# A two-layer hybrid decoder trunk: another start, 32 modulation tiles in another stage, and other buffers around the FFN

## The chip, the cores and the metric

The kernel runs on one core of a Trainium2 chip. A core has five engines with a queue each: TensorE (PE, matrix products), VectorE (DVE), ScalarE (ACT), GpSimd (POOL) and SyncE (SP, which here issues every DMA). Each engine takes its instructions strictly in the order in which they stand in its queue, and a wait stops all that stands behind it. PE writes to PSUM (eight banks of 128 x 512 fp32), the other data lies in SBUF. The metric is the device time of one execution in microseconds (us).

## The reference

All of it is fp32: 1024 tokens of width 1024, two layers, then a last RMSNorm.

```python
for l in range(DEPTH):
    mod = c_act @ ada_w[l] + ada_b[l]              # c_act = silu(c), one row
    shift1, scale1, gate1, shift2, scale2, gate2 = split(mod, 6)
    h = rms_norm(x, norm1_g[l]) * (1.0 + scale1) + shift1
    z = h @ w_in[l]                                # q | k | v | GLU input | two gates
    o = subln(diff_attention(rope(q), rope(k), v)) # 4 heads, two softmaxes each, causal
    y_attn = o @ w_attn_o[l]
    u = silu(layer_norm(conv31(ga * sigmoid(gb))))
    y_conv = u @ w_conv_o[l]
    x = x + (1 + gate1) * ((sig(g_attn)*y_attn + sig(g_conv)*y_conv) @ w_out[l])
    h2 = rms_norm(x, norm2_g[l]) * (1.0 + scale2) + shift2
    f_gate, f_up = split(h2 @ w_ffn_in[l], 2)      # 2 x 2816 columns
    x = x + (1 + gate2) * ((silu(f_gate) * f_up) @ w_ffn_out[l])
return rms_norm(x, final_g)
```

## The kernel before

Activations are kept transposed: eight feature tiles (128 features x 1024 tokens), each worked in two halves of 512 tokens (`hf`). Every fp32 operand of a product is split into a rounded high part and the rest (ACT makes the high part, DVE or POOL subtracts it), and three products are summed in one PSUM bank: high x high, high x low of the activation, low of the weight x high. A weight slab is 128 x 1024 (512 KB): `wslab` loads it into one of two `wraw` buffers, ACT casts `wh`, POOL subtracts `wl` (L139 to L142). A 128 x 512 output of 1024 inputs is thus 24 matmuls of 512 columns.

**Order of the work.** The program is written stage by stage, and a scheduler with a timing model of its own fixes the order in each engine's queue before the launch. It may pull an instruction ahead where its model finds the engine free, and tile pools set which buffer must be free first.

**Start (L503 to L538), layer 0.** x is loaded; ACT squares each tile by halves; DVE (half 0) and POOL (half 1) add the eight squares (L515); PE sums over partitions with a column of ones (`rstd_diag`, L307, 8 matmuls of one column); POOL raises to the power -0.5 (L310); DVE makes four diagonal tiles per half and PE spreads the factor over partitions (L317). Then, feature tile by feature tile: two modulation tiles (`ada_col`: a 512 KB load, and on DVE a 128 x 1024 multiply with accumulation by `cs` = silu(c), L193, a bias add L194, and for scales and gates one more column instruction), x times the factor (L532, DVE or POOL), ACT scales and shifts (L534) and casts `hh` (L535), DVE subtracts `hl` (L536). After it the rope tables: range reduction of angles on POOL in 76 small instructions (`rope_tables`, L210), two Sin on ACT, three small stores.

**GLU (L567 to L579).** Four slabs, kept at once, are multiplied by half (`linear_half`: the 16 products with `wh`, then the 8 with `wl`), then four more. In layer 0 the remaining 32 modulation tiles (16 to 47: gate1, shift2, scale2, gate2) stand behind it (L577). Convolution on DVE (31 taps, L614, with its sum in PSUM), attention and gate projections follow as one plan.

**Mix (L706 to L764).** `branch` multiplies attention and convolution outputs by their slabs (48 matmuls per slab); DVE multiplies each bank by a sigmoid gate (L749), POOL adds the two branches (L759), ACT and DVE split the sum (L762, L763). `w_out` follows (L806), DVE adds to x and squares are summed (L810, L302).

**FFN (L776 to L951).** One Strassen-like step: `b1`..`b7` are seven 512-feature operands; DVE and POOL form differences of the quarter tiles (L826 to L828, L834) and split them (L784), half of the tiles on each. 22 groups f each load two rows of slabs (`wraw`, `fraw`, two buffers each), form weight sums on DVE (L866 to L869) and make seven products of 12 matmuls (L880, L881, L883). Each group writes two 256 KB pieces to DRAM (`gf`).

**Output product (L954 to L1041).** `gblock` reads `gf` back in pieces (`gs`, 256 KB, five buffers) and splits them; all six blocks of half 0 are asked for ahead of the loop (L994), then eight x tiles (L996). 48 steps follow (two halves, two groups of four outputs, six blocks, two slabs), each up to 24 matmuls. Behind each of the first 16 steps of layer 0 stand three of layer 1's 48 modulation tiles (`ada_next`, L1022). The pools for `gs` and half of the blocks (`GP`) lie where the FFN's pools lay.

## Time and profile before

| | us |
|---|---|
| three timed runs | 2988.03, 2985.60, 2981.32; median 2985.60 |
| profiled execution, its own time | 2990.07 |
| its span, first to last instruction | 2988.2 |
| PE / DVE / ACT / POOL busy in the span | 2783.1 / 1836.9 / 1158.0 / 1719.9 |
| PE instructions | 12544 |
| granted TensorE clock, mean share | 0.965 |
| DMA, mean over the span | 118 GB/s |

Times in a trace count from the span's first instruction. Matmuls are pipelined and their ends are modelled, so PE's busy time also holds stretches in which it runs slowly. How well PE is used in a stretch is seen by its matmuls: their count against the length of the stretch.

### The profile page before, as it was taken

How to read it: one execution, taken by the hardware profiler on the slowest of the kernel's cores; microseconds unless marked ns; L12 is line 12 of the kernel's file. 1: busy time of each engine (PE TensorE's matmuls, PEld its weight loads, DVE VectorE, ACT ScalarE, POOL GpSimd, SP SyncE). 2: the span in 40 equal slices, each digit the busy share in tenths (PEclk: the TensorE clock that was granted, in tenths of full speed). 3: DMA queues.
4: the chain of work that ended last, by engine and by line, in shares of the span. 5: the costliest groups of instructions: out<-in, count | busy, mean ns of one | idle time of the engine just before them, and what ended most of it. 6: DMA issues, size and time to landing. Idle time of an engine off the chain costs nothing. (4 is left out here: it accounts for less than half of the span.)

```text
span 2988.2 us, 35455 instructions
## 1 busy us (share of the span) xinstructions
PE 2783.1 (93%) x12544; PEld 2284.7 (76%) x12544; DVE 1836.9 (61%) x2997; ACT 1158.0 (39%) x2059; POOL 1719.9 (58%) x1256
## 2 busy tenths in 40 slices
PE   3899999899979999889899999998997999998998
PEld 2688788777758888667788888886875788886886
DVE  8889976554574466589618989545446644443222
ACT  4246544343433333332322565435334233333321
POOL 6957745334686666554542776642457666666643
PEclk9999999989989999999999999998998999999999
DMA  7621222335232222388432122132451322225442
GB/s 272 229 83 65 71 78 85 113 102 194 100 110 88 78 85 85 112 277 287 158 121 89 64 75 78 56 107 85 141 201 68 119 85 85 85 78 180 136 121 93
DMA packets 151952, 353.92 MB, mean 118 GB/s; under 512 B 15328, under 2 KB 28000, under 8 KB 151776
## 3 DMA queue, kind: packets, MB, share of 16 engines
q1 hardware_dynamic: 151776, 351.67, 34.7%
q8 instruction: 99, 1.62, 0.2%
q14 instruction: 77, 0.63, 0.1%
HBM read 282.30 MB, written 69.30 MB: 118 GB/s over the span
## 5 line engine op out<-in xcount | busy, mean ns | idle before, releaser
L142 POOL TENSOR_TENSOR wl<-wraw,wh 128x1024 fp32r<-128x1024 f32 (+1 forms) x216 | 513.0, 2376 | 587.1 <-ACT wh L141 391.2
L141 ACT CAST wh<-wraw 128x1024 fp32r<-128x1024 f32 (+1 forms) x216 | 219.5, 1017 | 404.5 <-PE pfo L1018 186.7
L784 POOL TENSOR_TENSOR wt<-wraw,wt 128x512 fp32r<-128x512 f32 x172 | 247.7, 1441 | 169.6 <-ACT wt L783 169.5
L1017 PE MATMUL pfo<-gh,wh 128*128 128x512 f32 x640 | 256.1, 402 | 31.1 <-ACT gh L783 22.8
L151 PE MATMUL pg<-hl,wh 128*128 128x512 f32 x640 | 253.0, 397 | 16.9 <-DVE hl L536 16.8
L614 DVE SCALAR_TENSOR_TENSOR pc<-uc,vec,pc 128x512 f32<-128x512 f32 x348 | 261.1, 750 | 6.0
L150 PE MATMUL pg<-hh,wh 128*128 128x512 f32 x640 | 253.8, 401 | 9.1 <-ACT hh L535 8.9
L1018 PE MATMUL pfo<-gl,wh 128*128 128x512 f32 x640 | 254.3, 397 | 0.0
L1019 PE MATMUL pfo<-gh,wl 128*128 128x512 f32 x640 | 243.0, 399 | 8.7 <-POOL wl L142 8.6
L783 ACT CAST wt<-wraw 128x512 fp32r<-128x512 f32 x172 | 106.9, 622 | 310.2 <-PE pf L883 259.2
L609 POOL TENSOR_TENSOR uc<-uc,ct 128x512 f32<-128x512 f32 x120 | 139.0, 1158 | 57.5 <-ACT ct L608 56.8
L1017 PEld LDWEIGHTS pfo<-gh,wh 128*128 128x128 f32 x640 | 124.1, 194 | 60.9 <-ACT gh L783 23.7
L154 PE MATMUL pg<-hh,wl 128*128 128x512 f32 x640 | 168.7, 395 | 0.0
L443 ACT ACTIVATE e<-psc,nb 128x512 f32<-128x512 f32 (+2 forms) x192 | 110.5, 579 | 145.9 <-DVE nb L440 113.1
L1019 PEld LDWEIGHTS pfo<-gh,wl 128*128 128x128 f32 x640 | 123.3, 193 | 42.1 <-POOL wl L142 16.5
L151 PEld LDWEIGHTS pg<-hl,wh 128*128 128x128 f32 x640 | 121.0, 189 | 44.2 <-DVE hl L536 21.1
L150 PEld LDWEIGHTS pg<-hh,wh 128*128 128x128 f32 x640 | 121.8, 191 | 33.5 <-ACT hh L535 9.4
L1028 DVE SCALAR_TENSOR_TENSOR x<-pfo,gcol,x 128x512 f32<-128x512 f32 x32 | 23.7, 745 | 196.0 <-PE pfo L1019 195.5
L1018 PEld LDWEIGHTS pfo<-gl,wh 128*128 128x128 f32 x640 | 123.2, 192 | 25.9
L154 PEld LDWEIGHTS pg<-hh,wl 128*128 128x128 f32 x640 | 117.5, 188 | 23.3
L784 POOL TENSOR_TENSOR wt<-fraw,wt 128x512 fp32r<-128x512 f32 x88 | 118.7, 1349 | 26.9 <-ACT wt L783 26.9
L438 DVE TENSOR_REDUCE mx<-psc 128x1 f32<-128x512 f32 (+2 forms) x192 | 102.7, 549 | 23.8 <-PE psc L437 16.0
(324 smaller groups left out, 7652.3 us busy)
## 6 DMA issues: line engine op xcount, KB each, us to landing
wraw<-in_w_ffn_out_dram SPq DMA_DIRECT2D x80, 512.0 KB
wraw<-in_w_in_dram SPq DMA_DIRECT2D x72, 512.0 KB
adraw<-in_ada_w_dram SPq DMA_DIRECT2D x48, 512.0 KB
adraw<-in_ada_w_dram SPq DMA_DIRECT2D x96, 256.0 KB
fraw<-in_w_ffn_in_dram SPq DMA_DIRECT2D x44, 512.0 KB
wraw<-in_w_ffn_in_dram SPq DMA_DIRECT2D x44, 512.0 KB
gs<-gf SPq DMA_DIRECT2D x88, 256.0 KB
gd<-graw SPq DMA_DIRECT2D x64, 256.0 KB
```

The source lines that it names most:

```text
L141: S.copy(wh, raw)
L142: G.tensor_tensor(wl, raw, wh.bitcast(F32), op=ALU.subtract)
L150: PE.matmul(ps, wh[:, wc], rhs(0, k, hf), start=(k == 0), stop=False)
L151: PE.matmul(ps, wh[:, wc], rhs(1, k, hf), start=False, stop=False)
L154: PE.matmul(ps, wl[:, wc], rhs(0, k, hf), start=False, stop=(k == nk - 1))
L443: S.activation(e[:, n0:n1], pss[b][:, 0:n1 - n0], AF.Exp, bias=nb, scale=0.125, accum_out=sx[:, 2 * b + c:2 * b + c + 1])
L609: G.tensor_tensor(acc, acc, t, op=ALU.add)
L614: E.scalar_tensor_tensor(pc if k + 1 < CONV_K else acc, u[:, k:k + HF], w, pc, op0=ALU.mult, op1=ALU.add)
L784: E.tensor_tensor(lo, src, hi.bitcast(F32), op=ALU.subtract)
L1017: PE.matmul(ps, wh[:, wc], bh[:, k % 4, :], start=(not seen[q] and k == k0), stop=False)
L1018: PE.matmul(ps, wh[:, wc], bl[:, k % 4, :], start=False, stop=False)
L1019: PE.matmul(ps, wl[:, wc], bh[:, k % 4, :], start=False, stop=(seen[q] == NB - 1 and k == k1 - 1))
```

## The change

Seven edits, all in `trunk`:

1. The start takes all eight PSUM banks as one pool `ps0`, closed before the convolution; the four other PSUM pools open behind it. `pos` and `invf` are loaded first and the rope tables are written first.
2. ACT squares a whole tile and PE sums it at once: 8 one-column matmuls per tile, 64 in all, into one bank (`pst`). The adds of squares are gone. One power on POOL for both halves.
3. `cs` is a PSUM tile (two banks). Multiplication by factor and scale is one DVE instruction (L532's product is gone); half 0 takes `hl` on DVE, half 1 on POOL.
4. Behind each feature tile the first three GLU slabs take their 18 matmuls in six banks; the fourth slab and its product come later.
5. Modulation tiles 16 to 47 of layer 0 move into the mix, eight ahead of each of its first four rounds, with a second silu(c) in SBUF and three load buffers.
6. FFN opening: differences, and all splits of `b3`..`b7`, on DVE.
7. A pool on the right side (`ffnr`) stays open from the FFN to the layer's end: a third buffer for the second row of slabs, the five `gs` buffers, and two blocks; block 0 of half 0 is written in front of the last three FFN groups. x tiles are read during the first steps, and one `ada_next` stands behind each step in place of three.

```diff
+    pst0 = ExitStack()
+    ps0 = pst0.enter_context(tc.tile_pool(name="pstart", bufs=1, space=PSUM, reuse_waits="tile"))
...
-    cs0 = silu_c(ap0, 7)
-    Sqs = [nt("Sq") for hf in range(2)]
+    rope_tables(ap0)
+    pst = ps0.tile([P, KT], F32, name="pst", tag="s", bufs=6, padded_shape=[P, HF])
     for j in range(KT):
...
+        t = ap0.tile([P, T], F32, tag="sqt", name="sqt", bufs=2)
+        S.activation(t, xs[j], AF.Square)
+        for q in range(KT):
+            PE.matmul(pst[:, q:q + 1], t[:, q * P:(q + 1) * P], ones[:, 0:1], start=(j == 0 and q == 0), stop=(j == KT - 1 and q == KT - 1))
+    cs0 = silu_c(ap0, 7, ps0.tile([P, D], F32, name="cs", tag="cs", bufs=1))
...
     for j in range(KT):
+        if j < NS:
+            ws.append(glu_slab(0, j, up))
         for t in (KT + j, j):
             ada_col(0, t, cs0, ap0, 7)
...
-            (G if hf else V).tensor_tensor(xj, xj, pbs[hf], op=ALU.mult)
+            V.scalar_tensor_tensor(t, xs[j][:, hs], acol[0][0][:, j:j + 1], pbs[hf], op0=ALU.mult, op1=ALU.mult)
+            if hf:
+                S.activation(t, t, AF.Identity, bias=bc)
+                S.copy(hh.at(j), t)
+                G.tensor_tensor(hl.at(j), t, hh.at(j).bitcast(F32), op=ALU.subtract)
+            else:
+                S.activation(hh.at(j), t, AF.Identity, bias=bc)
+                V.scalar_tensor_tensor(hl.at(j), t, bc, hh.at(j).bitcast(F32), op0=ALU.add, op1=ALU.subtract)
+        for i in range(len(ws)):
...
+                for k in range(done[i], j + 1):
...
+                    PE.matmul(ps, wh[:, wc], hh, start=(k == 0), stop=False)
+                    PE.matmul(ps, wh[:, wc], hl, start=False, stop=False)
+                    PE.matmul(ps, wl[:, wc], hh, start=False, stop=(k == KT - 1))
...
-        if l == 0:
-            for t in range(16, 48):
-                ada_col(0, t, cs0, ap0, 7)
...
+        ada_t = iter(range(16, 48 if l == 0 else 16))
+        if l == 0:
+            csb = silu_c(B, 3)
         for j0 in range(0, KT + 2, 2):
+            for t in itertools.islice(ada_t, 8):
+                ada_col(0, t, csb, B, 3)
...
-                split_into(MV[p][0][:, j % 4, :], MV[p][1][:, j % 4, :], x, V if hf and j % 2 else G)
+                split_into(MV[p][0][:, j % 4, :], MV[p][1][:, j % 4, :], x, V if hf else G)
...
-            E = (V, G)[jj % 2]
+            E = V
...
-                split_into(MV[p][0][:, jj, :], MV[p][1][:, jj, :], x, V if jj % 2 else G)
+                split_into(MV[p][0][:, jj, :], MV[p][1][:, jj, :], x, V)
         xpool.close()
+        rst = ExitStack()
+        R = rst.enter_context(pool("ffnr", side="right"))
...
-                r2 = F.tile([P, D], F32, tag="fraw", name="fraw", bufs=2)
+                if self.f % 3 == 2:
+                    r2 = R.tile([P, D], F32, tag="rraw", name="rraw", bufs=1)
+                else:
+                    r2 = F.tile([P, D], F32, tag="fraw", name="fraw", bufs=2)
...
+            if g.f == FT - 4:
+                gb = [[gblock(0, 0)], []]
...
-                t = GP.tile([P, HF], F32, tag="gs", name="gs", bufs=5)
+                t = R.tile([P, HF], F32, tag="gs", name="gs", bufs=5)
...
-        gb = [[gblock(0, b) for b in range(NB)], []]
-        for j in range(KT):
-            DQ.dma_start(xs[j], xm[j])
+        gb[0] += [gblock(0, b) for b in range(1, NB)]
...
-                    for t in itertools.islice(ada_t, 3):
+                    for t in itertools.islice(ada_t, 1):
                         ada_next(t)
+                    if hf == 0 and jq == 0 and q == 0 and b >= 2:
+                        for j in range(2 * b - 4, 2 * b - 2):
+                            DQ.dma_start(xs[j], xm[j])
```

The scheduler's order follows the new text. Three places show it. The first is POOL's queue at the start; `ms` is the power of the first norm, `ropetmp` and `roper` belong to the rope tables, `wl` to a slab. Before:

```order
L120 MEMSET nhalf 128x8
L515 ISA
L515 TENSOR_TENSOR Sq<-Sq,sqt 128x512 x7
L310 TENSOR_TENSOR ms<-ms,nhalf 128x4 x2
L142 TENSOR_TENSOR wl<-wraw,wh 128x1024
L532 TENSOR_TENSOR x_87<-x_87,pb_233 128x512
```

Now, with 39 instructions of the rope tables and two `wl` ahead of the power:

```order
L227 TENSOR_TENSOR ropetmp<-ropetmp,roper 128x64
L240 TENSOR_TENSOR ropetmp<-ropetmp 128x64
L514 TENSOR_TENSOR ms_314<-ms_314,nhalf 128x8
L225 TENSOR_SCALAR roper<-ropetmp 128x64
L232 TENSOR_SCALAR ropetmp<-ropetmp 128x128
L140 TENSOR_TENSOR wl<-wraw,wh 128x1024
L226 TENSOR_SCALAR roper<-roper 128x64
```

The rope tables moved from behind the norm to both sides of its power; the remaining ones stand between the eight `hl` of half 1.

The second is DVE's queue at the end of layer 0's mix: `gin` is a gate times a branch, `m0l` and `m1l` are the low parts of the mixed tiles, `x` after `pwo` is the output of `w_out`. Before:

```order
L749 TENSOR_TENSOR gin<-py,gin 128x512
L763 TENSOR_TENSOR m0l_5821<-gin,m0h_5819 128x512
L763 TENSOR_TENSOR m1l_5825<-gin,m1h_5823 128x512
L810 SCALAR_TENSOR_TENSOR x_6409<-pwo,gcol_0_127,x_6409 128x512
L810 SCALAR_TENSOR_TENSOR x_6410<-pwo,gcol_0_127,x_6410 128x512
L302 TENSOR_TENSOR Sq<-Sq,sqt 128x512
```

Now:

```order
L796 TENSOR_TENSOR m1l_5693<-gin,m1h_5691 128x512
L192 SCALAR_TENSOR_TENSOR adraw,mod_112<-adraw,cs 128x1024
L193 TENSOR_TENSOR mod_112<-mod_112,vec 128x1
L192 SCALAR_TENSOR_TENSOR adraw,mod_112<-adraw,cs 128x1024
L204 TENSOR_SCALAR gcol_1_119<-mod_112 128x1
L193 TENSOR_TENSOR mod_112<-mod_112,vec 128x1
L204 TENSOR_SCALAR gcol_1_119<-mod_112 128x1
L843 SCALAR_TENSOR_TENSOR x_6434<-pwo,gcol_0_118,x_6434 128x512
L843 SCALAR_TENSOR_TENSOR x_6435<-pwo,gcol_0_118,x_6435 128x512
L301 TENSOR_TENSOR Sq<-Sq,sqt 128x512
```

All 32 multiplies (L192) stand in DVE's queue ahead of the first output of `w_out`, one or two between two gates.

The third is DVE's queue at the opening of layer 0's FFN; `x_6409` to `x_6416` are the eight tiles before, `x_6434` to `x_6441` the same now. Before:

```order
L827 TENSOR_TENSOR x_6411<-x_6415,x_6411 128x512
L828 TENSOR_TENSOR x_6415<-x_6415,x_6411 128x512
L784 TENSOR_TENSOR b7l<-x_6410,b7h 128x512
L784 TENSOR_TENSOR b5l<-x_6410,b5h 128x512
L784 TENSOR_TENSOR b5l<-x_6412,b5h 128x512
L834 TENSOR_TENSOR x_6414<-x_6414 128x512
L784 TENSOR_TENSOR b6l<-x_6414,b6h 128x512
L784 TENSOR_TENSOR b4l<-x_6414,b4h 128x512
```

Now:

```order
L861 TENSOR_TENSOR x_6440<-x_6440,x_6436 128x512
L867 TENSOR_TENSOR x_6438<-x_6438 128x512
L861 TENSOR_TENSOR x_6441<-x_6441,x_6437 128x512
L817 TENSOR_TENSOR b6l<-x_6438,b6h 128x512
L867 TENSOR_TENSOR x_6439<-x_6439 128x512
L817 TENSOR_TENSOR b7l<-x_6434,b7h 128x512
L867 TENSOR_TENSOR x_6440<-x_6440 128x512
L817 TENSOR_TENSOR b7l<-x_6435,b7h 128x512
L817 TENSOR_TENSOR b7l<-x_6436,b7h 128x512
L817 TENSOR_TENSOR b7l<-x_6437,b7h 128x512
```

From the norm's factor for half 1 to the last `b4l` DVE's queue holds 47 instructions in place of 29; POOL's holds 12 beside them in place of 29.

## Rows read from the trace of the kernel before

**Rows 1.** Stretches: length, busy us (count) by engine, clock, DMA share, GB/s
```profile
core 0: us, PE busy (x) PEld busy (x) DVE busy (x) ACT busy (x) POOL busy (x), PEclk, DMA share, GB/s
0.00:166.00 166.00, 105.85 (x417) 83.87 (x418) 141.10 (x277) 58.17 (x81) 116.89 (x112) 0.96 0.66 236
31.00:87.00 56.00, 30.18 (x109) 21.45 (x109) 56.00 (x112) 26.54 (x39) 41.31 (x31) 1.00 0.66 221
619.00:722.00 103.00, 103.00 (x455) 85.00 (x454) 51.83 (x69) 42.12 (x55) 44.97 (x18) 1.00 0.50 175
705.00:720.00 15.00, 15.00 (x68) 12.29 (x67) 6.19 (x7) 5.04 (x7) 5.28 (x3) 1.00 1.00 387
793.00:878.00 85.00, 61.63 (x222) 45.07 (x221) 62.21 (x63) 34.98 (x61) 65.24 (x45) 0.80 0.26 93
812.00:861.00 49.00, 35.28 (x125) 24.76 (x124) 36.61 (x30) 24.42 (x43) 43.39 (x29) 0.78 0.19 65
878.00:1251.00 373.00, 373.00 (x1647) 308.82 (x1645) 211.34 (x250) 117.04 (x194) 241.90 (x176) 1.00 0.24 81
1251.00:1351.00 100.00, 77.30 (x293) 59.94 (x292) 76.06 (x144) 30.91 (x44) 50.14 (x27) 0.85 0.81 269
1351.00:1480.00 129.00, 116.31 (x479) 93.38 (x478) 102.19 (x192) 38.17 (x51) 62.25 (x31) 0.93 0.69 226
2254.00:2339.00 85.00, 61.21 (x225) 44.90 (x224) 61.95 (x63) 34.86 (x61) 66.99 (x46) 0.84 0.26 92
2711.00:2737.00 26.00, 15.20 (x54) 11.62 (x52) 9.95 (x11) 10.75 (x18) 13.61 (x10) 0.74 0.71 227
```

**Rows 2.** Waits of PE from 0 to 166: total us, times, longest
```profile
PE pst L307 <- DVE subg L285: 19.7, 1, 19.7
PE pg L151 <- DVE hl L536: 16.8, 7, 11.6
...
PE pgb L154 <- POOL wl L142: 10.6, 2, 5.9
```

**Rows 3.** Timeline of DVE at the start: start us, us, instruction
```profile
38.03 1.21 DVE L193 SCALAR_TENSOR_TENSOR adraw<-adraw,cs 128x1024 f32<-128x1024 f32 x1
...
49.42 3.41 DVE L193 SCALAR_TENSOR_TENSOR adraw<-adraw,cs 128x1024 f32<-128x1024 f32 x1
...
86.81 0.67 DVE L536 TENSOR_TENSOR hl<-ht,hh 128x512 fp32r<-128x512 f32 x1
```

**Rows 4.** Timeline of POOL, 90 to 116
```profile
90.28 1.22 POOL L227 TENSOR_SCALAR roper<-roper 128x64 f32<-128x64 f32 x1
...
110.33 0.38 POOL L226 TENSOR_SCALAR roper<-ropetmp 128x64 f32<-128x64 f32 x1
...
113.68 2.34 POOL L142 TENSOR_TENSOR wl<-wraw,wh 128x1024 fp32r<-128x1024 f32 x1
```

**Rows 5.** Timeline of DVE in the mix, 645 to 650
```profile
645.10 0.69 DVE L763 TENSOR_TENSOR m0l<-gin,m0h 128x512 fp32r<-128x512 f32 x1 [1.06 <-ACT m0h L762]
...
646.70 2.83 DVE L763 TENSOR_TENSOR m1l<-gin,m1h 128x512 fp32r<-128x512 f32 x1
649.46 0.68 DVE L749 TENSOR_TENSOR gin<-py,gin 128x512 f32<-128x512 f32 x1
```

**Rows 6.** Waits of PE from 793 to 878, layer 0's FFN opening
```profile
PE pf L881 <- POOL b6l L784: 6.1, 1, 6.1
PE pf L880 <- ACT wt L783: 5.8, 1, 5.8
```

**Rows 7.** Timeline of DVE in that opening
```profile
833.60 1.75 DVE L784 TENSOR_TENSOR b7l<-x,b7h 128x512 fp32r<-128x512 f32 x1
```

**Rows 8.** Timeline of POOL in the same opening
```profile
838.12 1.70 POOL L784 TENSOR_TENSOR b6l<-x,b6h 128x512 fp32r<-128x512 f32 x1
```

**Rows 9.** Waits of PE from 1251 to 1480, layer 0's output product
```profile
PE pfo L1017 <- ACT wh L141: 15.4, 7, 5.1
PE pfo L1017 <- ACT gh L783: 12.0, 1, 12.0
```

More of the change, by code (lines that the diff above doesn't have):

```diff
@@ L101, in trunk @@
     xs = [xp.tile([P, T], F32, tag=f"x{j}", name=f"x{j}") for j in range(KT)]
+    invf = cp.tile([P, 1], F32, name="invf")
+    DQ.dma_start(invf, a["invf"])
+    pos_i = cp.tile([P, 64], I32, name="pos_i")
+    DQ.dma_start(pos_i, a["pos"])
     for j in range(KT):
@@ L504, in trunk @@
     ap0 = ust.enter_context(pool("ada0"))
[L505 to L506 removed]
+    rope_tables(ap0)
+    pst = ps0.tile([P, KT], F32, name="pst", tag="s", bufs=6, padded_shape=[P, HF])
     for j in range(KT):
[L508 to L520 removed]
+        t = ap0.tile([P, T], F32, tag="sqt", name="sqt", bufs=2)
[3 more added lines that the diff above has]
+    cs0 = silu_c(ap0, 7, ps0.tile([P, D], F32, name="cs", tag="cs", bufs=1))
+    ms = small("ms8", KT, 1)
+    V.tensor_scalar(ms, pst, 1.0 / D, 1e-6, op0=ALU.mult, op1=ALU.add)
+    G.tensor_tensor(ms, ms, nhalf, op=ALU.pow)
+    pbs = []
+    for hf in range(2):
+        dg = nt("dg")
+        for q in range(4):
+            V.tensor_scalar(dg[:, q * P:(q + 1) * P], ident, ms[:, 4 * hf + q:4 * hf + q + 1], None, op0=ALU.mult)
+        pb = rstd_spread(dg, ps0.tile([P, HF], F32, name="prn", tag="s", bufs=6), 4)
+        pbs.append(ap0.tile([P, HF], F32, name=f"pb{hf}", bufs=1))
+        S.copy(pbs[hf], pb)
     hs_parts = [hparts("h") for hf in range(2)]
     ws = []
+    NS = 3
+    start_ps = {}
+    done = [0] * NS
     for j in range(KT):
+        if j < NS:
+            ws.append(glu_slab(0, j, up))
         for t in (KT + j, j):
             ada_col(0, t, cs0, ap0, 7)
[L526 to L527 removed]
         for hf in range(2):
@@ L567, in trunk @@
         evs = [glu(c, True) for c in range(2)]
+        if l == 0:
+            for i in range(NS):
+                for hf in range(2):
+                    evs[i // 2][i % 2](hf, slice(hf * HF, hf * HF + HF), start_ps[i, hf])
+            pst0.close()
+            pm = top.enter_context(tc.tile_pool(name="pmain", bufs=2, space=PSUM, reuse_waits="tile"))
+            psc = top.enter_context(tc.tile_pool(name="pscore", bufs=SCB, space=PSUM, reuse_waits="tile"))
+            p1p = top.enter_context(tc.tile_pool(name="pone", bufs=8 - 3 - SCB, space=PSUM, reuse_waits="tile"))
+            pcv = top.enter_context(tc.tile_pool(name="pconv", bufs=1, space=PSUM, reuse_waits="tile"))
         for hf in range(2):
             hs = slice(hf * HF, hf * HF + HF)
-            for i in range(4):
+            for i in range(0 if l else NS, 4):
                 c = i // 2
@@ L936, in trunk, with gblock @@
         banks = itertools.cycle((psct, p1, psct, p1, psct, pct, pmt, pmt))
+        GP = [None]
+        NB = (FT + 3) // 4
+        def gblock(hf, b):
+            if b == NB - 1:
+                u = hunit("gt", GP[0], "G", 7)
+                un = [u[:, 0:2, :], u[:, 2:4, :]]
+            elif b == 0 and hf == 0:
+                un = [hunit(f"g{n}", R, "G0", 2) for n in "hl"]
+            elif b == 1 and hf == 1:
+                un = [hunit(f"g{n}", R, "G0", 2) for n in "hl"]
+            else:
+                un = [hunit(f"g{n}") if b >= 3 + hf else hunit(f"g{n}", GP[0], "G", 7) for n in "hl"]
+            for k in range(4 * b, min(4 * b + 4, FT)):
+                t = R.tile([P, HF], F32, tag="gs", name="gs", bufs=5)
+                DQ.dma_start(t, gf[k][:, HS[hf]])
+                split_into(un[0][:, k % 4, :], un[1][:, k % 4, :], t, V if k % 2 else G)
+            return un
         gs = [Group(f) for f in range(FT)]
@@ L985, in ada_next @@
             for h in range(2):
-                raw = GP.tile([P, HF], F32, tag="gs", name="adraw", bufs=5)
+                raw = R.tile([P, HF], F32, tag="gs", name="adraw", bufs=5)
                 DQ.dma_start(raw, a["ada_w"][l + 1, t][:, HS[h]])
@@ L1042, in trunk @@
         gst.close()
+        xpool.close()
+        rst.close()
+        xpool = ExitStack()
     xpool.close()
```

67 lines of the change are left out of this document (20 added, 47 removed).

## The prediction

> **What bounds the kernel now.** I read the stretches first [rows 1], then who PE waits for in the stretches where it falls behind, then single instructions. In the steady FFN, 878 to 1251, PE issues 1647 matmuls in 373 us, 0.2265 us each: that is PE at its pace at the full clock (1.00), nearly all of them of 512 columns. Against that pace the other stretches show what they lose. The kernel before loses
>
> - 79 us in 0 to 166, where the GLU's 384 matmuls are worth 87 us (the other 33 of the row are small ones);
> - 34.7 us in 793 to 878 and 34.0 in 2254 to 2339, the two FFN openings (222 and 225 matmuls worth 50.3 and 51.0);
> - 33.6 us in 1251 to 1351 and 20.5 in 1351 to 1480 (293 and 479 matmuls, worth 66.4 and 108.5), the output product of layer 0, and 13.8 in 2711 to 2737 at the opening of layer 1's.
>
> All these numbers are from [rows 1]. The mix, 619 to 722, loses nothing: 455 matmuls fill its 103 us. So PE sets the end, and an edit is worth what it gives back in the five losing stretches, less what it spoils in the mix.
>
> **The start.** PE first waits for the sums of squares, 19.7 us, then 16.8 us for low parts and later 10.6 us for two slabs' low parts [rows 2]. From 31 to 87 DVE is busy 56.0 of 56 us [rows 1] and the last low part starts at 86.81 [rows 3]. It is not only the norm that fills DVE: between those points its queue holds 21 multiplies, seven more than the norm still needs, pulled ahead by the scheduler: 7 x 1.21 = 8.5 us [rows 3], and one multiply of two SBUF tiles took 3.41 us beside POOL's large products. Now those multiplies are elsewhere, `cs` is in PSUM, and squares need neither DVE nor POOL. After the power, DVE has some six multiplies (7.3 us), 24 instructions on half tiles (at 0.69 [rows 5], 16.6) and 5 of small ones, 29 in sum. That would put the last feature near 62.
>
> But POOL is now in front of it. 39 rope instructions and two `wl` stand ahead of the power. A rope instruction took 0.38 us while DVE was still and 1.22 beside a working DVE, a `wl` 2.34 [rows 4]; so the power comes after 39 x 0.38 + 4.7 = 20 us of work at the least, 52 at the most. DVE has little to do that early, so I take 0.5 each, 24 us, plus some 5 until the positions are there and their angles formed: 29. Behind it stand 37 rope instructions and two more `wl` among the eight low parts of half 1; DVE works then, so 37 x 0.85, 4.7, and 8 x 1.7 [rows 8] give 50 us: the last low part near 79 in place of 87.5. What helps more is what is left then. Before, three slabs' products piled up behind the last feature; now 18 matmuls and the fourth slab's 48 remain, 66 x 0.2265 = 15 us, so four slabs are done at about 94. The other four slabs take 192 x 0.2265 = 43.5 us; before they also lost the 10.6 us to `wl`, which waited for the rope table; I leave 5. So the stretch ends at 143 in place of 166: 23 us given back. Ends: 8, if rope instructions stay near 1.22, and 38, if DVE alone sets the pace. The 64 one-column products cost nothing, since PE has no other work there.
>
> **The mix.** 32 multiplies at 1.21 us with about 0.36 of small column instructions are 50.2 us for DVE, in a stretch in which it has 103 - 51.8 = 51.2 us idle [rows 1]. All stand ahead of the first output of `w_out`, so what DVE lacks becomes PE's wait: PE's banks for four gates and three outputs cover a few us of it. Low end 0. For the high end: a subtraction of two SBUF tiles took 2.83 us where it met POOL, 0.69 alone, while a gate with a PSUM operand kept to 0.68 [rows 5]; `cs` lies in SBUF here, and 32 x 3.41 = 109 us would overrun by 58. POOL is busy 45 of the 103 us [rows 1], so 44% of the multiplies meet it and wait half a `wl`: 32 x 0.44 x 1.17 = 16 us; less some 4 that the banks cover, 12 us. The loads add 33 x 0.52 = 17.3 MB to the 175 GB/s x 103 us = 18 MB there: 343 GB/s, below the 387 that 705 to 720 shows [rows 1], but with little left; for that the high end stays.
>
> The Trainium skill, page "SBUF — State Buffer", section "Who interferes with whom", says that a DVE instruction with two SBUF inputs and a GpSimd instruction that reads SBUF exclude each other for the whole instruction. Rows 5 agree (2.83 against 0.69, and 0.68 with one input in PSUM). By it POOL's 45 us, the 39 us of multiplies and 22 us of other two-input work add to 106 us in 103: it speaks against this edit, and for a cost above nothing.
>
> **FFN openings.** PE waits 6.1 us for a low part that POOL makes, and 5.8 us for a weight that hangs on a late slab [rows 6]. DVE and POOL slow each other: 1.75 and 1.70 us for a split [rows 7, 8] that DVE alone does in 0.69 [rows 5]. From 812 to 861 POOL is busy 43.4 us with 29 instructions, DVE 36.6 with 30 [rows 1]. Now DVE's 47 at about 0.62 from start to start are 29 us, and POOL's 12, if each holds DVE up by 1.1 (1.75 less 0.65), 13: 42 in place of the 47 or so they took, 5 us earlier. The late slab gets its own buffer, so the 5.8 goes too, and group 2's products can fill the hole. I take 10 us for each layer, 20. Ends per layer: -3 (DVE becomes the only chain and PE's evacuations wait behind splits) and 18 (both waits and the clock, 0.80 in that stretch, come back). POOL's weight splits gain by it.
>
> The same rule of the Trainium skill ("SBUF — State Buffer", "Who interferes with whom") would, taken strictly, price POOL's 12 at their full 1.7 us: 29 + 20 = 49 us, and the gain from the splits would be nothing. That lies inside the ends.
>
> **Output product.** In layer 0 PE waits 12.0 us for the first split block and 15.4 for seven `wh` whose slabs come late [rows 9]. In front of them stood 22 `gf` pieces, eight x tiles and three modulation tiles per step. A step is 24 matmuls, 5.44 us, and three tiles of 512 KB with the slab are 2.1 MB: 386 GB/s, against 269 that came in 1251 to 1351 [rows 1]. One tile per step needs 193. Block 0 is split before the FFN ends and gives 10.9 us of work, in which block 1 must come. I count what stays lost: 12 us in the first 12 steps, since they also read 18 pieces, four more of half 1 and the x tiles (slabs 5.8, tiles 6.3, pieces 5.8, x 4.2: 22 MB, 82 us at 269 GB/s, 57 at 387, against 60 us of PE), 5 in the next 12, 4 in the rest: 21 of 54.1, so 33 given back (15 to 45). In layer 1 there is no modulation, and 13.8 fall to 3: 11 (5 to 13).
>
> **Sum.** -23 + 12 - 20 - 33 - 11 = -75 us. Against the profiled execution's own 2990.07 that is 2915; the median of the runs shown lies 4.5 us below it, so **2910**. With all low ends the sum is +36, with all high ends -132.
>
> **Rivals.**
> 1. *POOL binds the start.* The rope tables stand on both sides of the power, and rows 4 show them three times slower beside DVE. If they cost 1.2 us throughout, the power comes near 52 and the start gives 8 or nothing: 2910 + 19 = about 2929. Against it: DVE is idle early.
> 2. *The output product stays short of data.* 22 MB in the first 65 us need 339 GB/s, and that stage got 269 under load. Then layer 0 gives 13 and not 33: 2930. For it: seven waits for `wh` [rows 9]; against it: 387 in another stretch.
> 3. *Slower: the mix chokes.* Place: DVE's queue between the first gate and the first output of `w_out`. Each multiply waits for its load and for POOL, and holds the gates behind it; three load buffers make no reserve. The other four terms give 87, so it decides from 87 us, 2.7 us of wait per tile. With 3.4 us per tile, as the one slow multiply took in whole, 109 us are lost: 2985.6 - 87 + 109 = 3008. For it: the tight data rate and rows 3 and 5. Against it: DVE had 51 us idle.
> 4. *It does nothing:* the scheduler's new order in attention takes back what the start gives, and the openings stay; 2985.
>
> **Chances.** Forecast 0.58 (its own range 2880 to 2940), rivals 1 and 2 0.12 each, rival 3 0.07, rival 4 0.04, more than all this (below 2880) 0.07. What this kernel's runs can tell from no change is about 0.2%, 6 us. Faster 0.89, same 0.04, slower 0.07. The range 2868 to 2955 leaves out rivals 3 and 4 and the tails.
>
> **What would show it.** Right: the first keys' product starts near 143 in place of 166; the last low part of the norm is POOL's, near 79; gates in the mix keep their pace and PE loses about 12 us there; the opening's wait for `b6l` shrinks and the one for the late slab is gone; behind the FFN the first product of the output follows within 3 us. Wrong: POOL's power after 45; waits of PE for gates or for `m0h` of more than 30 us in the mix; GB/s above 330 with waits for `wh` after 1300; DVE saturated at the FFN opening with PE waiting for DVE's evacuations.

## The result, and the profile after

The changed kernel takes 2948.7 us (median of four runs, 2946.2 to 2949.1) against 2985.8 before: 37.1 us less, a ratio of 0.9876 with a 95% interval from 0.9859 to 0.9893. It is faster by more than the noise of the runs, and inside the stated range of 2868 to 2955, but above the forecast's own range (2880 to 2940): the gain is half of the 75 us that were forecast. The profiled execution spans 2947.3 us; before it was 2988.2.

Stretches of the changed kernel, with the columns of [rows 1] (length, busy us and count of each engine, granted clock, DMA share, GB/s). The three from 1225 to 1510 answer to a later comparison:

```profile
594.00:697.00 103.00, 86.53 (x363) 68.93 (x362) 102.72 (x160) 37.17 (x49) 47.40 (x16) 0.93 0.75 256
768.00:853.00 85.00, 72.43 (x282) 56.52 (x281) 66.24 (x83) 39.90 (x69) 45.16 (x30) 0.86 0.18 62
1225.00:1300.00 75.00, 65.92 (x267) 52.18 (x266) 41.74 (x63) 23.74 (x34) 44.40 (x24) 0.93 0.74 257
1300.00:1390.00 90.00, 76.97 (x290) 58.87 (x289) 60.13 (x115) 24.23 (x33) 42.92 (x22) 0.89 0.72 236
1390.00:1510.00 120.00, 108.56 (x454) 86.30 (x453) 81.11 (x168) 32.06 (x41) 50.21 (x23) 0.96 0.62 199
1251.00:1351.00 100.00, 83.42 (x314) 64.24 (x313) 66.60 (x118) 28.99 (x40) 51.53 (x26) 0.88 0.73 243
1351.00:1480.00 129.00, 112.03 (x451) 87.36 (x450) 100.57 (x213) 35.21 (x47) 55.11 (x27) 0.93 0.71 232
2240.00:2325.00 85.00, 71.85 (x289) 56.15 (x289) 71.08 (x87) 35.41 (x63) 51.91 (x33) 0.90 0.19 65
2677.00:2704.00 27.00, 23.52 (x103) 18.86 (x102) 10.89 (x8) 8.88 (x14) 17.26 (x10) 1.00 0.83 313
```

Against the pace of 0.2265 us per matmul, the mix now loses 103 - 363 x 0.2265 = 20.8 us (before 0); the FFN openings 21.1 and 19.5 (34.7 and 34.0); layer 0's output product 28.9 and 26.8 (33.6 and 20.5); the opening of layer 1's 3.7 (13.8). The start is shorter by 26.8 us: the first keys' product stands at 139.1 in place of 165.9. By term:

| term | forecast | measured |
|---|---|---|
| start | -23 | -26.8 |
| mix | +12 | +20.8 |
| two FFN openings | -20 | -28.1 |
| output product, layer 0 | -33 | +1.6 |
| output product, layer 1 | -11 | -10.1 |
| sum | -75 | -42.6 (the span: -40.9) |

Two of these rows depend on the window. The output product of layer 0 begins 24 us earlier in the changed kernel; taken from its own start over 283 us (1251 to 1534 before, 1227 to 1510 now) it loses 55.6 us (1004 matmuls) and 56.7 (999), so nothing was given back there either way. The row of layer 1 is its opening alone: over the whole stage (2711 to 2972 before, 2677 to 2931 now) the loss falls from 17.7 us (1074 matmuls) to 10.1 (1077), by 7.6.

The largest gain that was forecast did not come. In layer 0's output product PE still waits, where [rows 9] had 15.4 us for `wh` and 12.0 for the first split block. Waits of PE from 1251 to 1480 (total, times, longest):

```profile
PE pfo L1061 <- ACT wh L139: 17.4, 7, 4.9
PE pfo L1063 <- POOL wl L140: 11.9, 12, 1.6
```

The wait for the first block is gone. Waits for slabs, high and low part, have taken its place. SP's queue shows what stands around the slabs; its timeline in the changed kernel (start, us, instruction; xN counts the DMAs merged in a row; a slab is `wraw`, a half of a modulation tile `adraw`, an x tile `x<-xm`):

```profile
1234.85 0.38 SPq L135 DMA_DIRECT2D wraw<-in_w_ffn_out_dram  x1
1235.32 2.72 SPq L1070 DMA_DIRECT2D x<-xm  x5
1238.09 2.60 SPq L990 DMA_DIRECT2D gs<-gf  x4
1241.62 0.32 SPq L1070 DMA_DIRECT2D x<-xm  x1
1242.94 0.32 SPq L990 DMA_DIRECT2D gs<-gf  x1
1244.17 2.83 SPq L1070 DMA_DIRECT2D x<-xm  x2
1247.40 1.04 SPq L135 DMA_DIRECT2D wraw<-in_w_ffn_out_dram  x2
...
1446.07 0.39 SPq L135 DMA_DIRECT2D wraw<-in_w_ffn_out_dram  x1
1446.99 4.89 SPq L1033 DMA_DIRECT2D adraw<-in_ada_w_dram  x6
1451.98 0.39 SPq L135 DMA_DIRECT2D wraw<-in_w_ffn_out_dram  x1
1454.32 3.16 SPq L1033 DMA_DIRECT2D adraw<-in_ada_w_dram  x5
1457.58 7.40 SPq L135 DMA_DIRECT2D wraw<-in_w_ffn_out_dram  x3
```

The code has one tile, two halves, behind each slab, and two x tiles behind each of four steps, from the fifth on. The queue differs in two ways.

All eight x tiles stand in front of the fifth slab (the first four are issued at 1199, 1218 and 1235). In the kernel before they weren't in this stage at all. Its SP queue read them during the opening of the FFN, some 380 us earlier:

```profile
850.33 5.78 SPq L996 DMA_DIRECT2D x<-xm  x5
...
860.32 1.93 SPq L996 DMA_DIRECT2D x<-xm  x3
```

In layer 1 it is the same: 2310 to 2321 before, 2684 to 2694 now. So the change (its edit 7) brought 4.2 MB into the crowded start of each output product.

The modulation tiles first come late and then early. Counted over SP's timeline from the stage's first slab, the queue is 14 halves behind the code's place in front of the eighth slab, within three halves of it from the 13th to the 24th, and then ahead of it, by 26 in front of the 36th, where all 96 are issued. Up to seven halves stand between two slabs, where it catches up and again where it runs ahead. SP meanwhile stands with slabs behind it, as its waits from 1251 to 1480 say:

```profile
SPq L1033 <- DVE adraw L1034: 54.7, 38, 4.6
SPq L1033 <- DVE mod L1037: 23.9, 23, 3.5
```

Each is a load that waits until DVE frees one of the five `gs` buffers.

### The profile page after: what moved, and what is told of

It reads as the page before. It is cut to its first block, busy times and chain, and to the rows that moved or that the text cites. A ratio compares the mean times of both kernels' runs of the same rounds, so it can differ in the third digit from the quotient of the medians.

```text
span 2947.3 us, 35540 instructions
## 1 busy us (share of the span) xinstructions
PE 2799.7 (95%) x12656; PEld 2301.9 (78%) x12656; DVE 1875.3 (64%) x3026; ACT 1140.8 (39%) x2042; POOL 1640.2 (56%) x1212
## 5 line engine op out<-in xcount | busy, mean ns | idle before, releaser
L817 POOL TENSOR_TENSOR wt<-wraw,wt 128x512 fp32r<-128x512 f32 x172 | 238.9, 1393 | 146.8 <-ACT wt L816 144.9
L1061 PE MATMUL pfo<-gh,wh 128*128 128x512 f32 x640 | 258.3, 404 | 19.5 <-ACT wh L139 19.5
L1063 PE MATMUL pfo<-gh,wl 128*128 128x512 f32 x640 | 245.2, 404 | 13.4 <-POOL wl L140 13.2
L148 PE MATMUL pg<-hh,wh 128*128 128x512 f32 x592 | 235.8, 400 | 3.5 <-DVE d L686 3.4
L149 PE MATMUL pg<-hl,wh 128*128 128x512 f32 x592 | 234.1, 396 | 0.0
L1063 PEld LDWEIGHTS pfo<-gh,wl 128*128 128x128 f32 x640 | 123.9, 194 | 49.6 <-POOL wl L140 22.9
L152 PE MATMUL pg<-hh,wl 128*128 128x512 f32 x592 | 158.4, 396 | 0.0
L148 PEld LDWEIGHTS pg<-hh,wh 128*128 128x128 f32 x592 | 111.9, 189 | 26.2 <-issue 2.7
L149 PEld LDWEIGHTS pg<-hl,wh 128*128 128x128 f32 x592 | 111.9, 189 | 21.7
L152 PEld LDWEIGHTS pg<-hh,wl 128*128 128x128 f32 x592 | 108.1, 188 | 21.2
L636 ACT ACTIVATE ct<-uc,vec 128x512 f32<-128x512 f32 x120 | 86.7, 722 | 64.5 <-POOL uc L637 63.7
```

The costliest lines, as they stand in the source:

```text
L148: PE.matmul(ps, wh[:, wc], rhs(0, k, hf), start=(k == 0), stop=False)
L149: PE.matmul(ps, wh[:, wc], rhs(1, k, hf), start=False, stop=False)
L152: PE.matmul(ps, wl[:, wc], rhs(0, k, hf), start=False, stop=(k == nk - 1))
L817: E.tensor_tensor(lo, src, hi.bitcast(F32), op=ALU.subtract)
L1061: PE.matmul(ps, wh[:, wc], bh[:, k % 4, :], start=(not seen[q] and k == k0), stop=False)
L1063: PE.matmul(ps, wl[:, wc], bh[:, k % 4, :], start=False, stop=(seen[q] == NB - 1 and k == k1 - 1))
```

## Experiments

Time is the median in us; the ratio is to the kernel before, with its 95% interval. Since the scheduler moves other stages a little from kernel to kernel (the mix took 9.5 us longer in e2, where nothing of it was changed), the profiled executions are also compared by stretches. These are the starts of PE's first matmul of the keys (K), of the norm's spread behind layer 0's `w_out` (N), and of layer 1's `w_out` (W), read from each timeline; "edit" names what differs from the changed kernel. One profiled execution stands for each kernel, and the timed runs of one kernel lie up to 14 us apart, so a few us between two stretches prove little.

| run | edit | time | ratio | K to N | N to W | W to end |
|---|---|---|---|---|---|---|
| before | | 2985.8 | | 595.7 | 1399.2 | 827.4 |
| changed | | 2948.7 | 0.9876 (0.9859-0.9893) | 612.4 | 1388.1 | 807.7 |
| e1 | tiles pinned | 2930.9 | 0.9807 (0.9788-0.9826) | 609.6 | 1368.5 | 809.9 |
| e2 | no layer-1 modulation | 2915.6 | 0.9758 (0.9740-0.9775) | 621.9 | 1342.7 | 811.9 |
| e3 | multiplies alone | 2942.8 | 0.9850 (0.9835-0.9865) | 612.5 | 1378.6 | 811.1 |
| e4 | loads alone | 2930.2 | 0.9807 (0.9791-0.9824) | 612.6 | 1371.4 | 810.8 |
| e5 | three tiles per step | 2942.9 | 0.9853 (0.9837-0.9869) | 609.0 | 1382.8 | 806.8 |
| e6 | splits alternate | 2963.6 | 0.9924 (0.9909-0.9939) | 610.8 | 1395.0 | 818.0 |
| e7 | mix without tiles | 2922.5 | 0.9788 (0.9773-0.9802) | 589.8 | 1385.3 | 806.0 |
| e8 | pinned, later, x pinned | 2909.0 | 0.9744 (0.9726-0.9763) | 611.1 | 1352.5 | 802.1 |
| e9 | columns grouped in mix | 2941.9 | 0.9849 (0.9834-0.9864) | 606.9 | 1384.9 | 808.7 |
| e10 | e8 with columns grouped | 2908.9 | 0.9741 (0.9721-0.9760) | 607.6 | 1358.5 | 802.1 |
| e11 | e8, mix tiles spread | 2932.0 | 0.9812 (0.9791-0.9834) | 608.0 | 1385.8 | 803.4 |
| e12 | e8, x not pinned | 2929.6 | 0.9810 (0.9791-0.9828) | 611.0 | 1364.7 | 810.8 |

What layer 0's output product loses against 0.2265 us per matmul, in three stretches: us lost (matmuls). In the changed kernel they hold roughly the first 12 of the 48 steps, the next 12 and the rest. The windows are 1225 to 1300, to 1390 and to 1510; before they start at 1251 and in e2 at 1236, where those kernels' stage begins later.

| run | first, 75 us | second, 90 us | third, 120 us | sum |
|---|---|---|---|---|
| forecast left | 12 | 5 | 4 | 21 |
| before | 21.1 (238) | 21.6 (302) | 12.2 (476) | 54.9 |
| changed | 14.5 (267) | 24.3 (290) | 17.2 (454) | 56.0 |
| e1 | 14.5 (267) | 23.6 (293) | 0.6 (527) | 38.7 |
| e2 | 9.8 (288) | 0.5 (395) | -0.7 (533) | 9.6 |
| e3 | 13.4 (272) | 21.4 (303) | 12.6 (474) | 47.4 |
| e4 | 10.2 (286) | 25.7 (284) | 0.0 (530) | 35.9 |
| e5 | 14.3 (268) | 20.2 (308) | 15.1 (463) | 49.6 |
| e8 | 3.0 (318) | 19.3 (312) | 1.8 (522) | 24.1 |
| e12 | 9.5 (289) | 18.9 (314) | 4.0 (512) | 32.4 |

**e1, the tiles pinned to their steps.**

```diff
-                DQ.dma_start(raw, a["ada_w"][l + 1, t][:, HS[h]])
+                tc.keep_in_program_order(DQ.dma_start(raw, a["ada_w"][l + 1, t][:, HS[h]]))
```

> Each load of layer 1's modulation tiles is tied in SP's queue behind the slab of its own step, so that no tile runs ahead of its step; nothing else differs from the changed kernel (2948.7). Theory Order (the 33 us forecast for layer 0's output product were lost because the scheduler pulls 3 to 7 half tiles in front of a slab, although the code has one tile per step): the stage loses about 35 us in place of 57, time 2927 (2918 to 2935). Rival Rate (the stage is short of data over its whole length, in whatever order): no more than 6 us gained, 2943 or above. Rival Vector (the 96 multiplies slow the low parts on POOL): 2944 to 2950, and the waits for wl stay at about 12 us.

It took 2930.9, 17.8 us less; of the 20.7 us by which the profiled execution is shorter, 19.6 lie between N and W. The same bytes and multiplies in another order: the time is Order's, not Rate's or Vector's. The waits for `wl` fell too, from 11.9 to 5.4 us.

The gain isn't where the theory looked for it. Until 1300 e1's queue is like the changed kernel's, with five and seven halves between two slabs: there the tiles are late, and a pin doesn't bring them forward. From the 24th slab on each slab has its own two halves behind it, and the loss from 1390 to 1510 falls from 17.2 us to 0.6:

```profile
1390.00:1510.00 120.00, 119.20 (x527) 97.08 (x526) 89.94 (x165) 33.13 (x40) 55.59 (x28) 1.00 0.64 207
```

The multiplies read what the loads bring, so the pins hold them back in DVE's queue too; e1 doesn't part the two queues.

**e2, e3, e4: the price of the modulation and its two halves.** In e2 the loads and multiplies of the 48 tiles are left out; in e3 the loads alone, in e4 the multiplies:

```diff
 e3
-                DQ.dma_start(raw, a["ada_w"][l + 1, t][:, HS[h]])
-                V.scalar_tensor_tensor(raw, raw, 1.0, cs1[:, HS[h]], ...
+                V.scalar_tensor_tensor(raw, cs1[:, HS[h]], 1.0, cs1[:, HS[h]], ...
 e4
-                V.scalar_tensor_tensor(raw, raw, 1.0, cs1[:, HS[h]], ...
+                V.tensor_scalar(m2[:, h:h + 1], raw[:, 0:1], 1.0, None, op0=ALU.mult)
```

> The 96 loads and 96 multiplies of layer 1's modulation in layer 0's output product are left out (a sum of two columns stands in, so layer 1 is computed with another modulation). This is the whole price of the modulation there. If it causes the stage's 57 us of losses: 10 to 20 us stay, for the first blocks and the norm at the end, and the time is 2905 to 2912. If the gf pieces, x tiles and block order cause them: 2930 or above.

> The 96 multiplies stay, on the vector that lies in SBUF already, and the 96 loads of 256 KB are left out (layer 1 gets another modulation). Theory Loads (what hurts is the transfers, in front of the slabs or beside them): near the run without any modulation, 2905 to 2915. Rival Vector (DVE's two-input products and POOL hinder each other): 2930 or above, with 10 us or more of waits for wl.

> The 96 loads stay, and in place of each 512-column multiply DVE reads one column of what came (layer 1 gets another modulation), so buffers come free at once. Theory Loads: 2935 to 2949, the same waits for wh as in the changed kernel. Rival Vector, or a queue that stands because DVE frees buffers late: near the run without any modulation, 2905 to 2918.

Between N and W the modulation costs 45.4 us (1388.1 - 1342.7). That is nearly the stage's whole loss, so e2 holds by the stretch and misses its time by the mix. Multiplies alone cost 35.9 over e2, loads alone 28.7, so the harm of the two overlaps. My two theories both missed: e3 was expected near e2 by one, and e4 by the other; e3's time is Rival Vector's, but PE waits only 7.1 us for `wl` there, under the 10 that it named. By stretch, either alone loses in the second about what both lose, and e2 next to nothing. In the third the multiplies alone lose 12.6 us and the loads alone nothing, although they run as far ahead of the code (29 halves in front of the 35th slab): there, as far as these two runs show, the multiplies cost time and not the transfers that come early. SP's waits in e3, from 1226 to 1480, show one way:

```profile
SPq L135 <- POOL wl L140: 112.7, 27, 14.4
SPq L990 <- DVE mod L1036: 32.9, 6, 16.0
```

In e3 no tile is loaded, but each multiply still takes one of the `gs` buffers for its result, and a piece's load stood for 16.0 us in SP's queue behind a run of them; the next slab stood behind that load, and PE waited 6.7 us for a `wh` soon after. With loads alone SP stands for the ring's transfers instead (30.5 us, 26 times).

**e5, the code's spread undone.**

```diff
-                    for t in itertools.islice(ada_t, 1):
+                    for t in itertools.islice(ada_t, 3):
```

> The code's spread of layer 1's modulation alone is undone in the changed kernel: three tiles behind each of the first 16 steps in place of one behind each of 48. Theory Order (the scheduler pulled the tiles forward, so the spread never reached SP's queue): same within 8 us of the changed kernel's 2948.7, that is 2941 to 2957. Rival: the spread did give something, as the forecast had it: 2965 or above.

2942.9: it is 5.8 us faster than one tile per step. The time is theory Order's, but its reason isn't: the spread did reach the queue. With three tiles per step 72 halves stand in front of the 24th slab, with one 47, and from 1300 to 1390 DVE has 200 instructions in place of 115 and DMA moves 291 GB/s in place of 236:

```profile
1300.00:1390.00 90.00, 77.79 (x308) 60.52 (x309) 84.50 (x200) 20.45 (x25) 34.53 (x15) 0.92 0.87 291
```

The loss there is 4 us smaller, so the lower rate of the changed kernel was no gain in itself. Of e5's 15.1 us behind 1390, 9.6 are one wait for a split block (`gh`). As the scheduler places it, the spread gave nothing.

**e6, the FFN opening's splits back to both engines.**

```diff
-                split_into(MV[p][0][:, jj, :], MV[p][1][:, jj, :], x, V)
+                split_into(MV[p][0][:, jj, :], MV[p][1][:, jj, :], x, V if jj % 2 else G)
```

The other splits and the differences go back in the same way.

> The FFN openings' low parts and differences go back to alternating between DVE and POOL in the changed kernel; the late slab's own buffer stays. If the forecast's 10 us per layer come from DVE alone doing the splits, the time is about 2962 (the late slab's 5.8 us per layer stay won): 2955 to 2968. If POOL's share never held PE up: 2949. If the whole of the 14 us by which each opening lost less came from it: 2972 to 2977.

2963.6: 14.9 us back, 7.5 per layer, as the first case had it. PE's wait of [rows 6] returned to the tenth. The first row is e6's, from 767 to 853:

```profile
PE pf L919 <- POOL b6l L817: 6.1, 1, 6.1
```

and this is the largest of the changed kernel's there:

```profile
PE pf L919 <- DVE b3l L817: 4.3, 2, 2.8
```

The other 13 of the 28 us go by this with the late slab's wait (5.8 us in [rows 6]), which is gone in both; no run took its buffer back.

**e7, the mix without its tiles** (32 loads and multiplies left out; other columns stand in).

```diff
-                ada_col(0, t, csb, B, 3)
+                V.tensor_tensor(modb[0][:, t:t + 1], modb[0][:, t % 16:t % 16 + 1], vcol(0, t), op=ALU.add)
+                ada_use(0, t)
```

> The mix's 32 loads and multiplies of the modulation are left out of the changed kernel (other columns stand in for the results). Forecast term: 12 us; the trace after reads about 15 between the start's gain and the norm behind w_out. So 2934 (2930 to 2938). Rival: the tiles cost nothing and the 15 us are the new bank order's: 2946 or above. Rival chokes: more than 30 us come back, below 2918.

2922.5: the tiles cost 26 us, 22.6 of it between K and N, twice the forecast; not the 58 of the high end. Neither case of the expectation fits. DVE has no slack left in the mix, 102.7 busy of 103 us; e9 asks what fills it.

**e9, the small instructions grouped.** Each tile's bias, scale and gate were formed singly; here 8 columns at a time.

```diff
             V.scalar_tensor_tensor(raw, raw, 1.0, cs, op0=ALU.mult, op1=ALU.mult, accum_out=m)
+        if grouped:
+            if t % KT == KT - 1:
+                ada_use8(l, t // KT)
+            return
         V.tensor_tensor(m, m, vcol(l, t), op=ALU.add)
         ada_use(l, t)
```

> In the changed kernel's mix the small column instructions are grouped: each multiply's sum goes straight into its column, and the bias, the scale and the gate are formed for 8 columns at a time: 7 instructions in place of 56. The trace after has the 27 bias additions of that stretch at a mean of 0.61 us and 8 of the scales at 0.63, where one takes 0.15 undisturbed: some 23 us of DVE with the gates. Theory Columns (the mix's term came out at 17 to 26 in place of 12 because the small instructions wait beside POOL as the large ones do, and were priced at 0.36 per tile): 15 to 20 us come back, 2930 (2926 to 2936). Rival Multiplies (29 at 1.55 us, or their loads, set it): 2943 or above.

2941.9: 6.9 us, 5.5 of them between K and N. Theory Columns failed, and Rival Multiplies (2943 or above) is missed by 1 us. Groups of DVE from 594 to 697 (busy, mean ns of one), first the changed kernel, then e9:

```profile
L192 DVE SCALAR_TENSOR_TENSOR adraw<-adraw,cs 128x1024 f32<-128x1024 f32 x29 | 44.8, 1554 | 0.0
...
L193 DVE TENSOR_TENSOR mod<-mod,vec 128x1 f32<-128x1 f32 x27 | 16.4, 609 | 0.2
...
L796 DVE TENSOR_TENSOR m1l<-gin,m1h 128x512 fp32r<-128x512 f32 x7 | 4.8, 680 | 0.0
...
L204 DVE TENSOR_SCALAR gcol<-mod 128x1 f32<-128x1 f32 x10 | 1.3, 142 | 0.0
```

```profile
L192 DVE SCALAR_TENSOR_TENSOR adraw<-adraw,cs 128x1024 f32<-128x1024 f32 x32 | 55.6, 1754 | 2.2 <-DMA adraw<-in_ada_w_dram 2.2
...
L810 DVE TENSOR_TENSOR m1l<-gin,m1h 128x512 fp32r<-128x512 f32 x8 | 9.8, 1220 | 0.0
...
L203 DVE TENSOR_TENSOR mod<-mod,vec 128x8 f32<-128x8 f32 x3 | 0.5, 163 | 0.1
```

The small ones are gone, and the multiplies have grown from 1.55 to 1.75 us and the splits of `m1l` from 0.68 to 1.22. Most of the time was a wait for POOL, and other two-input instructions paid it instead. DVE in the changed kernel's mix:

```profile
676.10 3.35 DVE L192 SCALAR_TENSOR_TENSOR adraw<-adraw,cs 128x1024 f32<-128x1024 f32 x1
...
680.37 1.22 DVE L192 SCALAR_TENSOR_TENSOR adraw<-adraw,cs 128x1024 f32<-128x1024 f32 x1
...
693.67 2.33 DVE L193 TENSOR_TENSOR mod<-mod,vec 128x1 f32<-128x1 f32 x1
```

and POOL beside it:

```profile
675.11 3.25 POOL L792 TENSOR_TENSOR gin<-gin 128x1024 f32<-128x1024 f32 x1 [1.30 <-DVE gin L777]
...
692.69 3.29 POOL L792 TENSOR_TENSOR gin<-gin 128x1024 f32<-128x1024 f32 x1 [3.11 <-DVE gin L777]
```

POOL's sums end at 678.36 and 695.98. The slow multiply ends 1.09 us behind the first, about its own length; the one-column addition ends at 696.00, 0.02 behind the second. The gates (L204), which read one SBUF tile, keep to 0.14.

**e8, pinned, later, and x pinned:** e1, and the x tiles pinned, and tiles from the ninth step on.

```diff
+        ada_n = iter([0] * 8 + [1] * 16 + [2, 1, 1] * 8)
-                    for t in itertools.islice(ada_t, 1):
+                    for t in itertools.islice(ada_t, next(ada_n)):
-                            DQ.dma_start(xs[j], xm[j])
+                            tc.keep_in_program_order(DQ.dma_start(xs[j], xm[j]))
```

> As the pinned kernel (2930.9), and two things more: the x tiles are pinned to their steps too, and layer 1's modulation tiles start behind the eighth step, when the first half's pieces are through: none in steps 0 to 7, one in steps 8 to 23, then four in three steps. Theory Order: the first 65 us of the stage were crowded by x tiles, pieces and tiles, and the pinned kernel still waits 17 us there; half of it and its half-clock time come back: 2920 (2914 to 2926). Rival Vector: 96 multiplies cost what they cost, wherever they stand: 2928 to 2934.

2909.0, better than expected and the fastest kernel here: 2.6% under the kernel before. Its stretches over layer 0's output product:

```profile
1225.00:1300.00 75.00, 73.74 (x318) 59.12 (x317) 42.39 (x52) 27.64 (x40) 48.49 (x26) 1.00 0.84 285
1300.00:1390.00 90.00, 77.76 (x312) 60.30 (x311) 62.22 (x124) 26.23 (x37) 47.25 (x25) 0.92 0.68 227
1390.00:1510.00 120.00, 118.34 (x522) 96.91 (x521) 91.18 (x178) 32.81 (x40) 57.62 (x28) 1.00 0.68 226
```

It loses 3.0, 19.3 and 1.8 us, 24 in sum; the changed kernel loses 14.5, 24.3 and 17.2, 56 in sum, in the same stretches. In the first of them it moves more (285 GB/s against 257). Its SP queue there:

```profile
1269.19 0.38 SPq L135 DMA_DIRECT2D wraw<-in_w_ffn_out_dram  x1
1269.67 0.89 SPq L1033 DMA_DIRECT2D adraw<-in_ada_w_dram  x2
1270.61 0.90 SPq L1071 DMA_DIRECT2D x<-xm  x2
1274.63 0.38 SPq L135 DMA_DIRECT2D wraw<-in_w_ffn_out_dram  x1
```

One tile and at most two x tiles stand between two slabs: the spacing that the forecast took for granted, with the tiles starting eight steps later than it had them.

**e12, the x tiles' pins taken back from e8.**

> The pinned and later kernel (2909.0) with the pins of the x tiles taken back: the scheduler again puts eight x tiles of 512 KB between the fourth and the fifth slab of layer 0's output product, where the code has two behind each of four steps. It parts the 22 us between the pinned kernel (2930.9) and the later one. If the x tiles in front of the fifth slab make PE's first wait there (4.7 us in the pinned kernel, and the half clock that follows), 2914 to 2919. If the later start of the modulation tiles brought it all, 2906 to 2911. If the x tiles brought it all, 2925 or above.

2929.6: as in the third case, nearly all of e8's 22 us over e1 comes from the x tiles, and next to nothing from the later start as long as they are not pinned (1368.5 to 1364.7 between N and W); the x tiles pinned without the later start were not run. The first case, 5 to 10 us, was too small since the same line stands in layer 1: of the 21.0 us between the profiled e12 and e8, 12.2 are between N and W and 8.7 behind W. Behind W the three kernels with pinned x tiles took 802.1 to 803.4 us and the others with the changed FFN opening 806.0 to 811.9, so layer 1's share is 3 to 10 us. PE's first wait in layer 0 from 1225 to 1300 is, in e12,

```profile
PE pfo L1062 <- ACT wh L139: 5.0, 2, 4.7
```

and in e8

```profile
PE pfo L1062 <- ACT wh L139: 0.4, 2, 0.3
```

**e10, e8 with the columns grouped**, in the mix and the output product, by the diff of e9.

> The pinned and later kernel (2909.0) with the columns grouped by 8, in the mix and in layer 0's output product. By theory Columns 15 to 20 us in the mix and 2 to 5 in the output product: 2888 (2882 to 2896). By rival Multiplies: 2902 or above.

2908.9: nothing. The mix gains 3.6 us and the stretch behind it loses 6.0. Whether grouping helps is open within this.

**e11, e8 with the mix's tiles spread.** 16 stay in the mix, 16 go into `w_out`; `cs` needs a pool of its own, and to make room the FFN's pool opens only behind `w_out`.

```diff
-        ada_t = iter(range(16, 48 if l == 0 else 16))
+        ada_t = iter([*range(16, 24), *(8 * b + j for j in range(8) for b in (4, 3)), *range(40, 48)] if l == 0 else [])
-            for t in itertools.islice(ada_t, 8):
-                ada_col(0, t, csb, B, 3)
+            for t in itertools.islice(ada_t, 4 if j0 < KT else 0):
+                ada_col(0, t, csb, adp, 2, pin=True)
...
+                for t in itertools.islice(ada_t, 1):
+                    ada_col(0, t, csb, adp, 2, pin=True)
                 ps = psct("pwo")
...
+        adst.close()
+        F = fst.enter_context(pool("ffn"))
```

> The pinned and later kernel (2909.0), its small instructions as they were, with half of the mix's 32 tiles moved on: 16 in the mix, four per round, 8 in the first half of w_out and 8 in the second, each load pinned to its place; the vector lies in a pool of its own, with two load buffers. DVE is busy 45% of the 68 us behind the mix in the changed kernel. If the mix's price is DVE's time there: half of the 23 us and its half-clock time come back, 2893 (2887 to 2899). Rival: the tiles cost as much in w_out, or two buffers are too few: 2905 to 2915.

2932.0, 23 us slower than e8, and inconclusive on the mix: between K and N it is 3.1 us shorter, but PE then waits from 768 to 853 for

```profile
PE pf L924 <- ACT wt L818: 29.0, 3, 24.8
```

that is, for the FFN's weights, whose pool was moved; the two load buffers that the rival named were not tested apart. The mix's price with tiles in `w_out` and the pool in place was not measured.

## Why the prediction was wrong, step by step

**What bounds the kernel** was right: PE's losses by stretch account for the gain (-42.6 against -40.9). That they do so within 2 us is in part luck: the mix's window reads 4 us more than K to N (20.8 against 16.7), and the windows of layer 1 gain 5 us more than W to end (24.6 against 19.7), where the x tiles also cost.

**The start** was right, and rival 1 did not come. POOL's power starts at 35.08 (forecast 29, wrong if after 45), the last low part ends at 79.0 (forecast 79; the power was 6 us late and the way behind it 6 us shorter, so the exact number is luck):

```profile
35.08 1.67 POOL L514 TENSOR_TENSOR ms<-ms,nhalf 128x8 f32<-128x8 f32 x1
...
77.71 1.30 POOL L542 TENSOR_TENSOR hl<-ht,hh 128x512 fp32r<-128x512 f32 x1
```

PE waits for no `wl` from 0 to 139, so the 5 us left for that were not needed, and the stretch ends at 139 in place of 143.

**The mix** had the right mechanism and the wrong size: +12 forecast, 17 to 21 measured, and 26 the price by e7. The forecast gave the wait for POOL to the multiplies (1.72 us each with it; measured 1.55) and none to the small column instructions (0.36 per tile; the bias additions alone came to 0.61 each). PE waits where it was said it would, in front of `w_out`, from 594 to 700:

```profile
PE pwo L148 <- ACT m0h L795: 6.8, 3, 3.6
PE pwo L149 <- DVE m0l L796: 5.2, 2, 3.3
PE pwo L149 <- DVE gcol L204: 3.8, 1, 3.8
```

Without POOL, DVE's work in those 103 us would be 29 multiplies at 1.22, some 35 small ones at 0.15, 27 half-width products and splits at 0.68, and 20.1 for the PSUM gates: about 84 us with the vector, the one-input columns and the accumulator reads (1.2, 1.3 and 2.2). It took 102.7, so by this estimate POOL, busy 47.4 us, held it up for some 19. The Trainium skill, page "SBUF — State Buffer", section "Who interferes with whom", has a two-SBUF-input instruction of DVE and a GpSimd instruction that reads SBUF exclude each other, and says that issue order, not the shape, decides who blocks. The one-column addition of 2.33 us and e9 agree. The prediction set the rule against the multiplies and splits alone, but every two-input instruction shares the wait, a one-column addition too. POOL's whole time it isn't: the rest of the 47.4 us didn't hold DVE up.

**The FFN openings** gave 28 and not 20; e6 has 15 of it from the splits, and the rest goes with the late slab's wait.

**Layer 1's output product** gave 10 of 11 at its opening, and 7.6 over the whole stage, where the x tiles now stand.

**Layer 0's output product is the step that failed:** "One tile per step needs 193", with "33 given back". Nothing was given back: of the 54 us lost before, 21 were to stay, and 56 did. The step read the order of the code as the order of SP's queue, in two places.

The first is the x tiles. "In front of them stood 22 `gf` pieces, eight x tiles" follows the text of the loop (L996), but the queue before had read them at 850 to 862. So their 4.2 MB were new in this stage, and all in front of the fifth slab, where the sum had them spread over 12 steps, as bytes that had been there before. e12 against e8: 12.2 us in layer 0, 3 to 10 in layer 1.

The second is the tiles. The sum left 5 us in the second 12 steps and 4 in the rest; 24.3 and 17.2 were lost. Of the 17.2, e1 gives back 16.6 with the order enforced from the 24th slab on. The 24.3 are the modulation's, since e2 loses 0.5 there, but no order that was tried brought them below 18.9. The rate, on which "needs 193" rests, is not what held PE up: e5 moved 291 GB/s there and lost no more.

With both in their places (e8) N to W falls by 46.7 us against the kernel before, where the forecast for the opening and the output product of layer 0 was 43, and the stage loses 24 us where 21 were to stay. The sums are close in part by luck, since the stretches are 3, 19 and 2 us and not 12, 5 and 4. N to W also holds layer 1's stages up to its `w_out`, which the edits leave as they were. The order of SP's queue is fixed before any run, and the trace before showed where the x tiles stood; this step needed both, and argued from the loop instead.

**Rival 2** had the right stage and the wrong reason. It expected the stage to be short of data by rate. But the waits came at 243 and 232 GB/s, and e8 moves the same bytes with 24 us lost in place of 56. The stated sign, more than 330 GB/s with waits for `wh` after 1300, did not occur: no 10 us from 1300 to 1480 came over 322.

**Open:** why the modulation costs about 20 us from 1300 to 1390 in every order that was tried (in e8 PE waits there 8.1 us for `wl` and 3.9 for `wh`); which of the two queues, SP's or DVE's, e1 set right; what the x tiles would cost if they were read at the FFN opening again; and how much of the mix's 26 us could be had elsewhere.
